# Router products moved into the scan, logits by column groups, an unsplit first gather, dummy products in waits and modulation sums on VectorE

## The chip, the cores and the metric

One core of one Trainium2 chip runs the whole kernel as one program. The metric is the device time of that core in microseconds. A run of the kernel before took 1290.3 us in the median of three (1288.49 to 1298.68). The engines are named as in the profile: PE is TensorE (PEld its weight loads), DVE is VectorE, ACT is ScalarE, POOL is GpSimd, SP is the engine that issues the DMAs.

## The reference

A trunk of two layers over one sequence of 256 tokens with 1024 channels, in float32. Each layer has a token mixer and a channel mixer, each inside a normalisation, a shift and scale that come from a condition vector, a gate and a residual.

```python
cond = silu(c)
for i in range(2):
    mod = cond @ ada_w[i] + ada_b[i]
    sh1, sc1, g1, sh2, sc2, g2 = split(mod, 6)
    h = rmsnorm(x, norm_g[i, 0]) * (1 + sc1) + sh1
    y = mla_mixer(h) if i == 0 else mamba2_mixer(h)
    x = x + g1 * y
    h = rmsnorm(x, norm_g[i, 1]) * (1 + sc2) + sh2
    y = swiglu(h) if i == 0 else moe_swiglu(h)
    x = x + g2 * y
return rmsnorm(x, final_norm)

def moe_swiglu(h):                       # 8 experts, 2 for each token
    logits = h @ w_router
    top_vals, top_idx = top_k(logits, 2)
    gates = sum(one_hot(top_idx) * softmax(top_vals))
    return sum(gates[:, e:e+1] * swiglu_e(h) for e in range(8))
```

## The kernel before

The activations stand transposed, channels on partitions: `xT` holds 8 blocks of 128 channels by 256 tokens. Weights come from HBM in pieces of 1 MB through a ring of eight buffers (`raw`, ten in the experts); every load is issued on SP's queue in the order in which a scheduler lists it, and a load waits until its buffer's last reader is done. Precise products are made of three: a weight is split by ACT and DVE (line 158) into a high and a low half, and lines 346 to 348 or 1280 multiply high by high, high by low and low by high. A float32 product is one instruction in the program and two records in the trace. The order on each engine is the scheduler's; the code's order and the releases of buffers guide it.

**The start.** The modulation of the first sub-layer is needed in units of 512 columns: units 0 and 2 are shift and scale of channel blocks 0 to 3, units 1 and 3 of blocks 4 to 7. `ada_rows` (line 246) multiplies the condition with the weights on PE, each of the eight row blocks on one of four column groups of 32, so that the result is four partial rows; DVE copies it (line 249) and `ada_columns` (line 257) turns it into columns with a column that has a one in each group (`one4`). `make_gsc` and `normmod` (lines 268, 329, 331) then give the normalised blocks `h32`, and `win_mm` (line 437) projects them: six products a block, blocks 0 to 3 first, then units 1 and 3, then blocks 4 to 7. Rows for the sine and cosine, the latents (`latent`, lines 291, 486) and attention follow. Later modulation units are summed on DVE instead (line 219), beside PE's other work.

**The scan.** Layer 1's mixer goes over four groups of heads. Two PSUM banks called `s` serve decay steps, transposes and norms, two called `in` the projections, four called `y` the output sums.

**The router.** `ssm_out` of the last group ends the mixer; its last half calls `then(m)` before each of eight blocks of output channels: `finish` adds the residual (line 364), `logits` (line 981) multiplies a block of `xT` with the router's weights, 128 tokens by 8 experts a product, `token_rows` (line 991) transposes tokens onto partitions, and ACT sums their squares (line 995). Ahead of them stand, once, the logits of the shift (line 953: the modulation as weights, 8 columns), and the gains in a layout of one column a channel (line 966), all in one `in` bank. Then come the root and reciprocal (lines 1018 to 1020), the logits with their scale (1022), the two largest and their indices (1044, 1046), the choice `sel` (1049), ranks by five thin products (1064 to 1068), positions `pos` (1070) and the selection matrix of the first expert (1084).

**The first gather.** `halves_of` scales the transposed tokens and splits them into `xt_hi` (ACT, line 1054) and `xt_lo` (DVE, line 1055); ACT copies the tokens (1103); gates and the sorting of experts by their number of tokens follow on DVE (1105 to 1146). `gather` (line 1189) multiplies high and low halves with the selection, four products of 128 columns a block; the first expert has 64 slots and takes only 64 of them, which ACT brings out with gain and shift (1197). Its weights, in float32 and without splitting, are multiplied at line 1372. Eight of its 1 MB pieces are loaded during the last scan group (`early`), two more into the ring's extra buffers behind the router; the next load waits until the first buffer has been used up. The experts follow in a fixed order of slots (64; 128 and 32; 128 and 64; 128 and 128; 32).

Of the kernel before, what the change touches and what calls it, by code (L numbers as in the profile page):

```python
# [79 lines left out]
def body(ctx: ExitStack, tc, x, c, positions, ada_w, ada_b, norm_g,  # L80
# [112 lines left out]
    few = per.tile([P, 4], F32, name="few")  # L193
    warm, halfpi, zero, one4 = (few[:, i:i + 1] for i in range(4))
# [57 lines left out]
    def ada_columns(units, rows):  # L252

        ps = pt("m")
        for i, (u, row) in enumerate(zip(units, rows)):
            for m in range(4):
                PE.matmul(ps[:, 4 * i + m:4 * i + m + 1], row[:, m * P:(m + 1) * P], one4, start=i == m == 0,
                          stop=True, skip_group_check=True)
        for i, u in enumerate(units):
            V.tensor_add(mod[:, 0, 4 * u:4 * u + 4], ps[:, 4 * i:4 * i + 4], vecT[:, 0, 4 * u:4 * u + 4])  # L260
# [116 lines left out]
    with ExitStack() as lctx:  # L377
# [13 lines left out]
        V.reduce_sum(one4, ident.rearrange("p (g q) -> p g q", g=4)[:, :, 0], axis=AX.X)  # L391
# [8 lines left out]
        win = [win_load(0, 3), win_load(3, 3)]  # L400
        aw[1] = ada_load(0, 1)
        u3 = ada_w[0, :, 1536:2048]
# [21 lines left out]
        ada_columns((0, 2), [ada_rows(aw[u]) for u in (0, 2)])  # L424
# [16 lines left out]
        ada_columns((1, 3), [ada_rows(aw[u]) for u in (1, 3)])  # L441
# [240 lines left out]
    with ExitStack() as lctx:  # L682
# [221 lines left out]

        y = st = None
        for g in range(SG):
# [32 lines left out]
            if g >= 2:  # L939
                last_gate(8 + g)  # L940
        y2 = state(SG - 1, st)
# [3 lines left out]
        make_gsc(1, 1)  # L945
        ssm_out(SG - 1, 0, *y)


        A.activation(warm, zg[:, 3, 0:1], AF.Sqrt, scale=0.0)
        V.tensor_mul(wrg, wrt, gsc[:, 1, 1, :].unsqueeze(2).to_broadcast([P, DC, NE]))  # L950
        ps_lg = pt("in")
        for k in range(DC):
            PE.matmul(ps_lg[:, 2 * NE:3 * NE], mod[:, 1, 24 + k:25 + k].to_broadcast([P, P]), wrt[:, k, :],
                      start=(k == 0), stop=(k == DC - 1), skip_group_check=True)
        V.tensor_copy(lg0, ps_lg[:, 2 * NE:3 * NE])


        scr = nrm.tile([P, 512], F32, tag="acc", name="scr")
        m24, ssq = scr[:, :24], scr[:, 32:38].rearrange("p (z j) -> p z j", z=3)
        SP.dma_start(m24, consts[:, C_EIGHTH:NCONST])  # L960
        gs8 = nrm.tile([P, 2, P], F32, tag="tt", name="gs8")
        for z, src in enumerate((gsc[:, 1, 1, :], mod[:, 1, 24:32])):
            V.tensor_tensor(gs8[:, z, :].rearrange("p (k a) -> p k a", k=DC),
                            src.unsqueeze(2).to_broadcast([P, DC, 16]),
                            m24[:, 0:16].unsqueeze(1).to_broadcast([P, DC, 16]), ALU.mult)
            PE.matmul(ps_lg[:, (3 + z) * NE:(4 + z) * NE], gs8[:, z, :], m24[:, 16:24], start=False, stop=True,
                      skip_group_check=True)
# [30 lines left out]
        def then(m):  # L998
# [4 lines left out]
            if m == 5:  # L1003
                logits(0)
            if m == 6:
                token_rows(0)
# [675 lines left out]
```

## Time and profile before

| | us |
|---|---|
| runs of the kernel, median (lowest, highest) | 1290.3 (1288.49, 1298.68) |
| profiled execution, its own time | 1296.65 |
| its span, first to last instruction | 1294.9 |
| mean granted PE clock in it | 0.967 |
| PE, DVE, ACT busy | 1220.2, 838.6, 692.0 |
| HBM read | 405.46 MB, 314 GB/s over the span |

Times in the rows below are from the start of the span. A row of a chain gives start, length and what the chain went through; a row of a timeline start, busy time, engine, line, operation, output and inputs, and in brackets the idle time before it with what ended it. A row by windows gives for each engine the busy time and, in brackets, the number of instructions, then the granted PE clock (1.00 is 2.4 GHz, 0.50 is 1.2 GHz), the share of the DMA engines and GB/s. A busy PE need not be at its peak, since products overlap.

### The profile page before, as it was taken

The numbers are of one execution on the slowest core, as the hardware profiler recorded it, in microseconds if no ns is written. First come the engines' busy times: TensorE is split into PE (matmuls) and PEld (weight loads), VectorE is DVE, ScalarE is ACT, GpSimd is POOL, SyncE is SP. The second block draws the span as 40 slices with busy tenths as digits, with TensorE's granted clock in tenths as the row PEclk, the third lists the DMA queues.
The fourth block names the chain that finished last, engine by engine and source line by source line (L and its number), as shares of the span: only waits on it lengthen the run. The fifth ranks groups of instructions, "written<-read, shape, count | busy, mean of one in ns | idle before, by whom it ended". The sixth has DMA issues, their size and how long they took to land.

```text
span 1294.9 us, 21688 instructions
## 1 busy us (share of the span) xinstructions
PE 1220.2 (94%) x8510; PEld 985.2 (76%) x8510; DVE 838.6 (65%) x1293; ACT 692.0 (53%) x1156; POOL 16.9 (1%) x16
## 2 busy tenths in 40 slices
PE   6999999999999999998999997899999999999975
PEld 4678899999989999996548884388855688888731
DVE  3377788778779788863037880288912779988412
ACT  2368554555467776634147660377703676776301
POOL 4000000000000000000000000000000000000000
PEclk8999989999989999997999998999999999999989
DMA  9786559888943356424999999999999999998895
GB/s 343 274 305 215 195 191 380 295 304 282 326 148 131 130 198 243 179 99 164 421 421 420 421 384 416 421 421 420 403 386 421 420 420 386 379 353 315 339 421 213
DMA packets 104748, 407.99 MB, mean 315 GB/s; under 512 B 10417, under 2 KB 16062, under 8 KB 70974
## 3 DMA queue, kind: packets, MB, share of 16 engines
q1 hardware_dynamic: 104638, 406.53, 81.3%
q8 instruction: 68, 1.11, 0.4%
q14 instruction: 42, 0.34, 0.1%
HBM read 405.46 MB, written 1.05 MB: 314 GB/s over the span
## 4 chain that ended last, share of the span: by engine, by line
PE 80%; DMA 11%; ACT 4%; DVE 3%; issue 1%; SPq 0%; ACTq 0%; DVEq 0%
PE a L1280 19%; PE y L1325 10%; DMA raw<-in_moe_w_down_dram 7%; PE a L1372 6%; DMA raw<-in_moe_w_up_dram 4%; PE y L346 3%; PE gu L347 3%; PE gu L346 3%; PE gu L348 3%; PE y L347 3%; PE y L348 3%; PE in L348 2%; PE in L346 2%; PE in L347 2%; PE mm L437 2%; PE mm L504 2%
## 5 line engine op out<-in xcount | busy, mean ns | idle before, releaser
L158 DVE TENSOR_TENSOR wlo<-raw,whi 128x1024 fp32r<-128x1024 f32 x395 | 466.6, 1218 | 87.9 <-ACT whi L158 86.3
L158 ACT CAST whi<-raw 128x1024 fp32r<-128x1024 f32 x395 | 404.2, 1051 | 189.7 <-PE a L1280 42.8
L1280 PE MATMUL a<-wlo,xe_hi 128*128 128x512 f32 (+1 forms) x464 | 154.3, 346 | 0.2
L1280 PE MATMUL a<-whi,xe_lo 128*128 128x512 f32 (+1 forms) x464 | 153.3, 342 | 0.0
L1280 PE MATMUL a<-whi,xe_hi 128*128 128x256 f32 (+1 forms) x464 | 111.8, 346 | 7.8 <-ACT whi L158 7.8
L219 DVE SCALAR_TENSOR_TENSOR acc<-raw,cond,acc 128x512 f32<-128x512 f32 x140 | 103.2, 748 | 3.2 <-ACT acc L217 1.5
L346 PE MATMUL gu<-hT_hi,whi 128*128 128x256 f32 x352 | 99.8, 284 | 1.2 <-ACT hT_hi L333 1.2
L1280 PEld LDWEIGHTS a<-wlo,xe_hi 128*128 128x128 f32 x464 | 87.8, 189 | 16.2 <-DVE wlo L158 3.4
L347 PE MATMUL gu<-hT_lo,whi 128*128 128x256 f32 x352 | 99.8, 284 | 0.0
L348 PE MATMUL gu<-hT_hi,wlo 128*128 128x256 f32 x352 | 99.2, 282 | 0.0
L1280 PEld LDWEIGHTS a<-whi,xe_lo 128*128 128x128 f32 x464 | 88.1, 190 | 10.0
L1280 PEld LDWEIGHTS a<-whi,xe_hi 128*128 128x128 f32 x464 | 76.4, 189 | 24.3 <-ACT whi L158 15.0
L1372 PE MATMUL a<-raw,xe 128*64 128x384 f32 (+3 forms) x640 | 81.6, 415 | 0.0
L346 PE MATMUL in<-hT_hi,whi 128*128 128x256 f32 (+1 forms) x264 | 76.0, 288 | 0.7 <-DVE r L302 0.7
L348 PE MATMUL in<-hT_hi,wlo 128*128 128x256 f32 (+1 forms) x264 | 75.5, 287 | 0.5 <-DVE wlo L158 0.5
L1293 DVE TENSOR_TENSOR sg<-sg,a 128x512 f32<-128x512 f32 (+2 forms) x30 | 18.1, 639 | 87.9 <-PE a L1372 76.0
L347 PE MATMUL in<-hT_lo,whi 128*128 128x256 f32 (+1 forms) x264 | 74.7, 283 | 0.0
L1372 PEld LDWEIGHTS a<-raw,xe 128*64 128x64 f32 x640 | 46.0, 136 | 34.6 <-issue 26.4
L1439 PE MATMUL a<-raw,xe 128*32 128x128 f32 (+1 forms) x960 | 54.6, 363 | 18.2 <-DMA raw<-in_moe_w_up_dram 18.2
L346 PEld LDWEIGHTS gu<-hT_hi,whi 128*128 128x128 f32 x352 | 67.2, 191 | 1.4 <-ACT hT_hi L333 1.4
L347 PEld LDWEIGHTS gu<-hT_lo,whi 128*128 128x128 f32 x352 | 67.3, 191 | 0.0
L348 PEld LDWEIGHTS gu<-hT_hi,wlo 128*128 128x128 f32 x352 | 67.3, 191 | 0.0
(407 smaller groups left out, 2359.6 us busy)
## 6 DMA issues: line engine op xcount, KB each, us to landing
raw<-in_moe_w_gate_dram SPq DMA_DIRECT2D x88, 1024.0 KB, 7.4
raw<-in_moe_w_up_dram SPq DMA_DIRECT2D x88, 1024.0 KB, 14.6
raw<-in_moe_w_down_dram SPq DMA_DIRECT2D x85, 1024.0 KB, 16.0
raw<-in_ada_w_dram SPq DMA_DIRECT2D x46, 1024.0 KB, 7.3
raw<-in_ssm_w_in_dram SPq DMA_DIRECT2D x20, 1024.0 KB, 5.2
raw<-in_ffn_w_down_dram SPq DMA_DIRECT2D x11, 1024.0 KB, 8.6
raw<-in_ffn_w_gate_dram SPq DMA_DIRECT2D x10, 1024.0 KB, 8.0
raw<-in_ffn_w_up_dram SPq DMA_DIRECT2D x10, 1024.0 KB, 8.8
```

The costliest lines, as they stand in the source:

```text
L158: return A.copy(hi, src), V.tensor_sub(lo, src, hi)
L219: V.scalar_tensor_tensor(acc, w[k // 4][:, k % 4, :], cond[:, k:k + 1], acc, op0=ALU.mult, op1=ALU.add)
L346: PE.matmul(ps, whi, ahi, start=(first and i == 0), stop=False, skip_group_check=skip)
L347: PE.matmul(ps, whi, alo, start=False, stop=False, skip_group_check=skip)
L348: PE.matmul(ps, wlo, ahi, start=False, stop=(last and i == n - 1), skip_group_check=skip)
L437: PE.matmul(ps, win[k // 3][:, k % 3, sl], h32[:, k, :], start=first and k == 0, stop=k == DC - 1, skip_group_check=True)
L504: PE.matmul(ps, lhs(k), rhs(k), start=(k == 0), stop=(k == n - 1))
L1280: PE.matmul(bank[:, o:o + n], a[:, j, :], w[:, m], start=f, stop=l, skip_group_check=True)
L1293: V.tensor_mul(self.sg[:, sl], self.sg[:, sl], self.acc["u", b][:, :n])
L1325: PE.matmul(self.y[b], a, w[:, b * 512:(b + 1) * 512], start=f, stop=l, skip_group_check=True)
L1372: PE.matmul(bank[64 * h:64 * (h + 1), o // 2:(o + n) // 2], self.xhi[:, j, :], w[:, h, :], start=first, stop=last, skip_group_check=True)
L1439: PE.matmul(self.acc[which, b][32 * g:32 * g + 32, o:o + m * P], self.xhi[:, j, :], w[:, first - q0::2, :, h], start=j == 0 and c % 2048 = ...
```

## The change

- The router's work that needs no token (gain times router weights, the logits of the shift, the gains in their layout) moves into the first group of the scan as `router()`, in an `s` bank. The shift's logits are summed over blocks by DVE first, so that one thin product is left of eight.
- The logits take the router's weights as the stationary side: 8 columns on one of four column groups, 256 tokens streaming, four blocks a call. The four partial sums, transposed, are copied to SBUF and folded by two thin products.
- The first gather uses the scaled tokens whole in float32 (`xt`), 64 columns, two products a block. The split into halves, the gates and their sorting go behind it.
- `keep_warm` puts products of ones with ones into waits: 34 at the start, 13 between the logits and the first gather.
- The sums of the first four modulation units go from PE to DVE, with ACT taking the first block, in two accumulators a unit; `ada_pair` (line 263) adds them in thin products. The loads are in another order: units 1 and 3 ahead of the second and third part of `w_in`.
- The PSUM banks of the experts are laid out with `y` first.

```diff
-    def ada_rows(w):
-        ps = pt("mm")
-        for k, wk in enumerate(t[:, k, :] for t in w for k in range(t.shape[1])):
-            g = k % 4 * 32
-            PE.matmul(ps[g:g + 32, :], cond[:, k:k + 1].to_broadcast([P, 32]), wk, start=k < 4, stop=k >= 4,
-                      skip_group_check=True)
-        row = nrm.tile([P, 512], F32, tag="acc", name="row")
-        V.tensor_copy(row, ps)
-        return row
+    def ada_sums(w):
+        both = hlp.tile([P, 1024], F32, tag="wlo", name="acc2")
+        acc = [both[:, z * 512:(z + 1) * 512] for z in range(2)]
         for k, wk in enumerate(t[:, k, :] for t in w for k in range(t.shape[1])):
+            a = acc[k % 2]
+            if k == 0:
+                A.activation(a, wk, AF.Copy, scale=cond[:, k:k + 1])
+            elif k == 1:
+                V.tensor_scalar(a, wk, cond[:, k:k + 1], None, op0=ALU.mult)
+            else:
+                V.scalar_tensor_tensor(a, wk, cond[:, k:k + 1], a, op0=ALU.mult, op1=ALU.add)
+        return acc
+    def ada_pair(u, sums, warm=(0, 0)):
         ps = pt("m")
+        for i, acc in enumerate(sums):
+            if warm[i]:
+                keep_warm(pt("mm"), warm[i])
+            for z in range(2):
+                for m in range(4):
+                    c = 4 * i + m
+                    PE.matmul(ps[:, c:c + 1], acc[z][:, m * P:(m + 1) * P], ones[:, 0:1],
+                              start=z == 0 and c == 0, stop=z == 1, skip_group_check=True)
...
+    def keep_warm(ps, n):
+        for _ in range(n):
+            PE.matmul(ps[:, 384:], ones, ones, start=True, stop=True, skip_group_check=True)
...
-        win = [win_load(0, 3), win_load(3, 3)]
+        win = [win_load(0, 3)]
         aw[1] = ada_load(0, 1)
-        aw[3] = [load(u3[0:512, :], 4), load(u3[512:768, :], 2), load(u3[768:1024, :], 2)]
-        win += [win_load(6, 2)]
+        aw[3] = ada_load(0, 3)
...
+        win += [win_load(3, 3), win_load(6, 2)]
...
-        ada_columns((0, 2), [ada_rows(aw[u]) for u in (0, 2)])
+        sums = ada_sums(aw[0]), ada_sums(aw[2])
+        ada_pair(0, sums, (8, 26))
...
-        ada_columns((1, 3), [ada_rows(aw[u]) for u in (1, 3)])
+        sums = ada_sums(aw[1]), ada_sums(aw[3])
+        ada_pair(1, sums)
...
+        def router():
+            make_gsc(1, 1)
+            V.tensor_mul(wrg, wrt, gsc[:, 1, 1, :].unsqueeze(2).to_broadcast([P, DC, NE]))
+            ps = pt("s")
...
+            SP.dma_start(m24, consts[:, C_EIGHTH:NCONST])
+            V.tensor_mul(by_k, wrt, mod[:, 1, 24:32].unsqueeze(2).to_broadcast([P, DC, NE]))
+            V.reduce_sum(sums, by_k.rearrange("p k n -> p n k"), axis=AX.X)
+            PE.matmul(ps[:, 0:NE], ones, sums, start=True, stop=True)
...
+            V.tensor_copy(lg0, ps[:, 0:NE])
+            V.tensor_copy(gain8, ps[:, NE:3 * NE].rearrange("p (z e) -> p z e", z=2))
...
         def logits(k0):
-            for k in (k0, k0 + 1):
-                for j in range(2):
-                    PE.matmul(ps_lg[:, j * NE:(j + 1) * NE], xT[:, k, j * P:(j + 1) * P], wrg[:, k, :],
-                              start=False, stop=(k == DC - 1), skip_group_check=True)
+            for i in range(4):
+                PE.matmul(ps_lg[32 * i:32 * i + NE, 0:S], wrg[:, k0 + i, :], xT[:, k0 + i, :], start=k0 == 0,
+                          stop=k0 > 0, skip_group_check=True)
...
+        token_rows(6)
         logits(4)
-        token_rows(6)
-        logits(6)
+        lgT = nrm.tile([P, S], F32, tag="tt", name="lgT")
+        V.tensor_copy(lgT, ps_lg[:, 0:S])
         V.tensor_add(ssq[:, 0, :], ssq[:, 0, :], ssq[:, 1, :])
+        dim = pt("y")
+        keep_warm(dim, 2)
+        for j in range(2):
+            PE.matmul(ps_lg[:, S + j * NE:S + (j + 1) * NE], lgT[:, j * P:(j + 1) * P], fold, start=True, stop=True,
+                      skip_group_check=True)
+        keep_warm(dim, 8)
...
+    for (q, j), ps in pst.items():
+        A.activation(xt[:, j, :, q * 64:(q + 1) * 64], ps.rearrange("t (p c) -> t c p", c=DC), AF.Copy,
+                     scale=rtok[:, j:j + 1])
...
+    keep_warm(dim, 3)
...
-    for cc in range(DC):
-        gather(xs, psel, cc, True)()
+    for c0 in (0, 4):
+        ps = pt("a").rearrange("p (c t) -> p c t", c=4)
+        for cc in range(c0, c0 + 4):
+            for j in range(2):
+                PE.matmul(ps[:, cc - c0, 0:n0], xt[:, j, cc, :], sel0[:, j, :], start=j == 0, stop=j == 1,
+                          skip_group_check=True)
+        for cc in range(c0, c0 + 4):
+            A.activation(xs[0][0][:, cc, :], ps[:, cc - c0, 0:n0], AF.Identity, bias=gain8[:, 1, cc:cc + 1],
+                         scale=gain8[:, 0, cc:cc + 1])
```

On DVE at the start, before, where `row` is the copied modulation row and `tt` a normalised block ahead of its shift:

```order
L709 CAST ej<-cst 128x128 x2
L415 RECIPROCAL r<-r 128x2
L210 COPY vecT<-n 128x128
L249 COPY row<-mm 128x512 x2
L260 TENSOR_TENSOR mod<-m,vecT 128x4 x2
L268 SCALAR_TENSOR_TENSOR gsc<-mod,vecT 128x4
L329 SCALAR_TENSOR_TENSOR tt<-xT,gsc,n 128x256 x2
```

On DVE at the same place now, where `acc_182` and `acc_191` are the accumulators of units 0 and 2, `acc_294` and `acc_303` of units 1 and 3:

```order
L720 CAST ej<-cst 128x128 x2
L249 TENSOR_SCALAR acc_182<-raw,cond 128x512
L424 RECIPROCAL r<-r 128x2
L251 SCALAR_TENSOR_TENSOR acc_182<-raw,cond,acc_182 128x512
L210 COPY vecT<-n 128x128
L251 SCALAR_TENSOR_TENSOR acc_182<-raw,cond,acc_182 128x512 x5
L249 TENSOR_SCALAR acc_191<-raw,cond 128x512
L251 SCALAR_TENSOR_TENSOR acc_191<-raw,cond,acc_191 128x512 x6
L266 TENSOR_TENSOR mod<-m,vecT 128x2x4
L210 COPY vecT<-n 128x21
L279 SCALAR_TENSOR_TENSOR gsc<-mod,vecT 128x4
L340 SCALAR_TENSOR_TENSOR tt<-xT,gsc,n 128x256 x4
```

Two copies have become fourteen passes over 512 columns ahead of the first `mod`.

On PE behind the last output products of the scan, before (`in` is the bank of the logits, `sel` the choice):

```order
L981 MATMUL in<-wrg,xT 128x8 x6
L991 MATMUL in<-cst,xT 128x128
L991 MATMUL y<-cst,xT 128x128
L991 MATMUL in<-cst,xT 128x128
L991 MATMUL y<-cst,xT 128x128
L981 MATMUL in<-wrg,xT 128x8 x2
L1064 MATMUL y<-sel,uones 128x8
L1065 MATMUL y<-sel,uones 128x8
L1066 MATMUL y<-sel,uones 128x8
L1067 MATMUL y<-sel,uones 128x8
L1068 MATMUL y<-sel,uones 128x8
L1189 MATMUL a<-psel,xt_hi 128x128
```

On PE at the same place now (`lgT` is the copied transposed logits, `scr` holds the fold matrix, `ones` rows are the dummies):

```order
L999 MATMUL in<-xT,wrg 8x256 x3
L271 MATMUL y<-ones 128x128 x3
L1039 MATMUL in<-scr,lgT 128x8 x2
L271 MATMUL y<-ones 128x128 x7
L1086 MATMUL y<-sel,uones 128x8
L1087 MATMUL y<-sel,uones 128x8
L1088 MATMUL y<-sel,uones 128x8
L1089 MATMUL y<-sel,uones 128x8
L1090 MATMUL y<-sel,uones 128x8
L271 MATMUL y<-ones 128x128 x3
L1503 MATMUL a<-psel,xt 128x64 x16
```

The last group of logits is four products (three stand in its row here, one ahead of the transposes) instead of eight, ten dummies and the fold stand in front of the choice's products and three behind them, and the gather is sixteen products of 64 columns instead of 32 of 128.

## Rows read from the trace of the kernel before

**Rows 1.** The page's chain of waits, shares of the span by engine

```profile
PE 80%; DMA 11%; ACT 4%; DVE 3%; issue 1%; SPq 0%; ACTq 0%; DVEq 0%
```

**Rows 2.** By windows, around the router and in the first expert

```profile
577.00:582.20 5.20, 5.20 (x33) 5.19 (x32) 1.79 (x5) 0.00 (x0) 0.00 (x0) 0.68 0.02 3
...
592.50:602.70 10.20, 8.72 (x37) 8.19 (x37) 8.52 (x40) 7.53 (x17) 0.00 (x0) 0.50 0.68 256
602.70:606.20 3.50, 3.50 (x11) 1.01 (x12) 0.00 (x0) 1.69 (x2) 0.00 (x0) 0.50 0.00 0
...
625.00:650.00 25.00, 25.00 (x193) 14.99 (x191) 3.09 (x9) 3.61 (x11) 0.00 (x0) 1.00 1.01 420
```

**Rows 3.** The chain of waits through the router and the first expert

```profile
575.73 1.68 PE in L953 x16
...
583.11 0.79 PE in L981 x8
...
590.29 0.57 ACT junk L995 x3
...
591.67 0.36 DVE lg L1022 x2
...
592.78 0.18 DVE sel L1049
...
594.27 0.18 DVE pos L1070
...
594.68 0.28 DVE psel L1084
...
595.68 7.11 PE a L1189 x31
602.79 41.52 PE a L1372 x317
...
648.76 19.83 DMA raw<-in_moe_w_down_dram
```

**Rows 4.** Timeline of SP: the first load that needs a used buffer

```profile
606.39 0.33 SPq L132 DMA_DIRECT2D raw<-in_moe_w_gate_dram  x1
```

**Rows 5.** The chain of waits at the start

```profile
23.12 14.84 PE mm L437 x48
37.96 2.71 PE mm L246 x24
...
43.51 1.07 PE m L257 x8
...
46.21 9.84 PE mm L437 x36
```

**Rows 6.** By windows, at the start

```profile
8.00:22.00 14.00, 12.11 (x70) 6.82 (x69) 2.45 (x9) 5.38 (x10) 5.57 (x7) 1.00 1.05 391
...
24.00:29.00 5.00, 5.00 (x12) 2.92 (x12) 0.00 (x0) 0.52 (x2) 0.00 (x0) 0.50 1.05 384
...
46.00:50.00 4.00, 3.79 (x10) 3.06 (x11) 3.79 (x13) 1.46 (x4) 0.00 (x0) 0.57 1.05 392
```

**Rows 7.** Groups by line: the logits (count, busy us, mean ns, idle)

```profile
L981 PE MATMUL in<-wrg,xT 128*128 128x8 f32 x32 | 3.8, 245 | 0.0
```

**Rows 8.** Timeline of ACT behind the reciprocal

```profile
591.60 1.26 ACT L1054 ACTIVATE xt_hi<-s,rtok 128x512 fp32r<-128x512 f32 x2 [0.23 <-DVE rtok L1020]
...
593.89 1.09 ACT L1103 COPY x_tok<-s 128x512 f32<-128x512 f32 x2
...
596.92 1.28 ACT L1106 ACT_TABLE_LOAD   x1
```

**Rows 9.** One line's instructions: DVE's step of a modulation sum (ns least, median, most)

```profile
L219 DVE SCALAR_TENSOR_TENSOR acc<-raw,cond,acc x140: 732/748/803, 67.3 to 514.1; 128x512 f32<-128x512 f32 x140
```

**Rows 10.** Timeline at the start: ACT's copies, PE's wait for unit 2

```profile
11.87 1.54 ACT L421 COPY xT<-mm 128x512 f32<-128x512 f32 x3
...
18.64 0.14 PEld L246 LDWEIGHTS mm<-raw,cond 128*32 128x32 f32 x4 [0.42 <-DMA raw<-in_ada_w_dram]
```

More of the change, by code (lines that the diff above doesn't have):

```diff
@@ L192, in body @@
     V.memset(eps_t, EPS)
-    few = per.tile([P, 4], F32, name="few")
-    warm, halfpi, zero, one4 = (few[:, i:i + 1] for i in range(4))
+    few = per.tile([P, 3], F32, name="few")
+    warm, halfpi, zero = few[:, 0:1], few[:, 1:2], few[:, 2:3]
     V.memset(zero, 0.0)
@@ L940, in body @@
                 last_gate(8 + g)
+            if g == 0:
+                router()
         y2 = state(SG - 1, st)
@@ L944, in body @@
         y = y2
-        make_gsc(1, 1)
         ssm_out(SG - 1, 0, *y)
         A.activation(warm, zg[:, 3, 0:1], AF.Sqrt, scale=0.0)
[L950 to L955, printed above, removed]
-        scr = nrm.tile([P, 512], F32, tag="acc", name="scr")
[L959 to L967, printed above, removed]
-        V.tensor_copy(gain8, ps_lg[:, 3 * NE:5 * NE].rearrange("p (z e) -> p z e", z=2))
+        scr = nrm.tile([P, 512], F32, tag="acc", name="scr")
+        ssq, fold = scr[:, :6].rearrange("p (z j) -> p z j", z=3), scr[:, 8:8 + NE]
+        V.reduce_sum(fold, ident.rearrange("p (g q) -> p q g", g=4)[:, 0:NE, :], axis=AX.X)
         pst = {}
@@ L1135, in body @@
     by_rank(pos_s, pos)
-    by_rank(gates_s, gates)
-    split(ej[:, :, S:S + NE], ej[:, :, S + NE:S + 2 * NE], gates_s)
     cmx = ep.tile([P, 1], F32, name="cmx")
@@ L1180, in gathered, with gather @@
                 ew.tile([P, DC, P], F32R, tag="xe_lo", name="xe_lo"))
-    def gather(xs, sel2, cc, first=False):
+    def gather(xs, sel2, cc):
         m = len(xs) * P
@@ L1499, in body @@
     xs = [gathered(0)]
-    for cc in range(DC):
-        gather(xs, psel, cc, True)()
+    n0 = SLOTS[ORDER[0][0]]
+    sel0 = psel.bitcast(F32)[:, :, 0, 0:n0]
+    for c0 in (0, 4):
[3 more added lines that the diff above has]
+                PE.matmul(ps[:, cc - c0, 0:n0], xt[:, j, cc, :], sel0[:, j, :], start=j == 0, stop=j == 1,
+                          skip_group_check=True)
+        for cc in range(c0, c0 + 4):
+            A.activation(xs[0][0][:, cc, :], ps[:, cc - c0, 0:n0], AF.Identity, bias=gain8[:, 1, cc:cc + 1],
+                         scale=gain8[:, 0, cc:cc + 1])
+    V.tensor_sub(wts[:, :, 0:1], top[:, :, 1:2], top[:, :, 0:1])
+    A.activation(wts[:, :, 1:2], wts[:, :, 0:1], AF.Exp)
+    V.tensor_scalar(wts[:, :, 0:1], wts[:, :, 1:2], 1.0, None, op0=ALU.add)
+    V.reciprocal(wts[:, :, 2:3], wts[:, :, 0:1])
+    V.tensor_mul(wts[:, :, 3:4], wts[:, :, 1:2], wts[:, :, 2:3])
+    for j in range(2):
+        V.tensor_scalar(gates[:, j, :], m12[:, j, 0, :], wts[:, j, 2:3], None, op0=ALU.mult)
+        V.scalar_tensor_tensor(gates[:, j, :], m12[:, j, 1, :], wts[:, j, 3:4], gates[:, j, :],
+                               op0=ALU.mult, op1=ALU.add)
+    by_rank(gates_s, gates)
+    split(ej[:, :, S:S + NE], ej[:, :, S + NE:S + 2 * NE], gates_s)
+    for j in range(2):
+        A.copy(xt_hi[:, j, :, :], xt[:, j, :, :])
+        V.tensor_sub(xt_lo[:, j, :, :], xt[:, j, :, :], xt_hi[:, j, :, :])
     SP.dma_start(fn_row, bcast(final_norm, D))
```

72 lines of the change are left out of this document (23 added, 49 removed).

## The prediction

> **What bounds the kernel now.** I read the chain of waits first: PE holds 80% of it, DMA 11% [rows 1]. Both come to the same statement about time: nearly everything before the experts is PE in sequence, and behind the router the weight stream and PE go on together. So a stretch counts only if PE or the stream stands still in it, or PE runs slowly. A table by windows, read second, finds three such stretches around the router: PE's clock has a mean of 0.68 from 577.0 to 582.2, is 0.50 (the lower of its two levels, 1.2 GHz) from 592.5 to 602.7, and is 0.50 still to 606.2, while the DMA engines rest completely in that last window [rows 2]. Later the stream runs at 420 GB/s [rows 2], and the first expert ends in a 19.8 us wait for weights [rows 3]. That is why the router is worth its whole length: all buffers are full, the next weight load is issued at 606.39, when the first buffer has been used up [rows 4], and whatever moves that issue moves the stream and all that hangs on it.
>
> The fourth place is the start. There PE carries the chain from 23.12 on, but 8.3 us of it (37.96 to 46.21) are modulation rows, their column products and the way back to the next normalised block [rows 5], and two stretches have a mean clock of 0.50 and 0.57 [rows 6].
>
> **Frame.** The profiled execution took 1296.65 us, 1294.9 of them span. The sum below is of differences inside it. The median of the runs shown is 1290.3, 6.35 lower; I carry the differences over to that median unchanged.
>
> **The router, up to the choice of experts.** Sixteen thin records of the shift logits leave PE's path: 1.68 us [rows 3]. Four more (the gains) at the same 0.105 each leave: 0.4. They go into the scan (below). Behind them the clock falls: 5.2 us at a mean of 0.68 are 1.66 us lost [rows 2]. With dense products in their place I let that go: 1.6. The logits were 32 thin records [rows 7] at 0.79 us for eight [rows 3], 3.2 in all. They become eight products of 256 columns, two groups of four, each on a column group of its own. The modulation rows before are of that form, 24 records of 512 columns in 2.71 us [rows 5], so 0.9 for a group of four products (eight records) and 0.45 for one half as wide. The second group is broken by transposes and by the last residual; I charge 1.4 together, which saves 1.8. Serial they would be 3.6 (a product of 256 columns has two records of about 0.22: 36 in 9.84 us [rows 5], 3.6 us of them at half clock), a loss of 0.4. The fold is new: copy of the transposed logits (0.4), dummies, two thin products (0.4), handovers (0.3). It stands beside the last squares, the root and the reciprocal, which take from 590.29 to 591.67 [rows 3]; the two paths end within 0.2 us of each other, and I charge 0.2 (0 to 1). Together 2.1 + 1.6 + 1.8 - 0.2 = 5.3 us until the choice is made.
>
> The Trainium skill, "TensorEngine Tiling (Array Packing)", section Key Properties, says that a change of tiling mode drains TensorE, which speaks against logits in column groups between full-width products. The rows show no gap at such a change: the 32-column rows start in the chain at 37.96, exactly where the full-width products end (23.12 + 14.84) [rows 5]. If each of some five changes cost 0.2 us, what DVE stands between two of its steps at 594.45 [rows 3], the forecast below would be 1.0 us later; by the rows it stays.
>
> **From the choice to the first gather.** Before, the choice ends at 592.96 and the gather's unbroken run begins at 595.68: 2.7 us. DVE's own steps in it, positions and selection, are 0.18 and 0.28 [rows 3]; the rest is five thin products at half clock and the low halves of the gathered rows, which DVE takes in between. The low halves go. What stays is the thin products at full clock (0.5), handovers (0.3), positions 0.2, one small copy 0.1, the selection 0.4: 1.5. Gain 1.2.
>
> **The gather.** 32 products of 128 columns at half clock were 7.1 us [rows 3]. Now 16 float32 products of 64 columns, 32 records, at the 0.1 us of a thin record at full clock [rows 3]: 3.4 to 3.5. No row shows this form; at half clock it would be 6.8. ACT is a second limit: four scalings of 0.63, four copies of 0.55, a table load of 1.28 and an exponential stand before its first evacuation [rows 8], 6.6 us from the reciprocal. That ends 0.2 behind PE's way, so I credit 3.4.
>
> **The first buffer.** From 602.79 [rows 3] to the next issue at 606.39 [rows 4] are 3.6 us at half clock, so 1.8 at full: gain 1.8. The sum of the router is 5.3 + 1.2 + 3.4 + 1.8 = 11.7 us; the issue that stands at 606.39 would come near 594.7. Gates, the split of the gathered rows and the final part of the sorting move behind the gather; the first expert keeps PE 41 us before it needs them, so that cover is ample, and if it were gone their DVE and ACT work would cost about 5 us.
>
> **In the scan.** Six thin records (0.65 us) go onto PE, which is the bound there. The four small DVE products, one reduction and two copies stand between weight splits that wait for ACT or PE, and I count them as hidden; without that cover they are 1.7 us. The load of the 24 constants moves forward in SP's queue, in front of weight loads that wait for buffers in any case. Charge 0.7 (0.4 to 2.5).
>
> **The start.** The sums now run on DVE: seven steps a unit, 748 ns each as the same step elsewhere [rows 9], and ACT's step in front. ACT is free at 13.41 [rows 10]; plus about 0.6 for its step, 14.0. Then 0.3 + 6 x 0.75 for unit 0 and 7 x 0.75 for unit 2: 24.05. The last of these weights lands at 18.64 [rows 10], so DVE sets it, not the transfer. A last thin group 1.07 [rows 5], then the way from there to PE (44.58 to 46.21, 1.63 [rows 5]) and a small copy: first product at 26.9, where it was 23.12. That is a loss of 3.8. DVE starts the second pair at about 28.9 and ends it at 38.65. PE has three chunks before that, 36 records, not 48: 7.7 us at full clock, 11.1 at the mean of 14.84 for 48 [rows 5], so it is done at 34.6 to 38.0. Then come 32 thin records, the last eight behind DVE. PE is free for the fourth chunk at 40.0 to 42.2, I take 41.0, and done with it at 43.8. The old kernel is at the same point at 46.21. Gain 2.4: a later first half repaid by work that stands beside PE instead of on it. The second and third part of the projection's weights now stand behind all modulation weights; at 384 GB/s [rows 6] some 11.5 MB behind the input land near 38, 3 us before they are needed. Late next is ACT: PE comes to the first sum of squares near 49, and ACT, with a table load of 1.28 [rows 8] and sine and cosine in front, has the squares near 50; for that I credit no more than 2.4. Bounds: with no fall of the clock at either place of rows 6, +5.3; with the lower level throughout, a loss of 18 (third rival). The 18 dummies start at 13.5 and end by 17.5 at full clock, ahead of the sum they wait with, so they cost nothing; at half clock they end at 21 and do.
>
> **Sum.** 11.7 + 2.4 - 0.7 = 13.4; 1290.3 - 13.4 = **1276.9 us**. All behind the first expert is shifted as a whole, since the stream, its buffers and PE start it in the state they had before.
>
> **Rivals.** (1) The clock falls in the wait for the choice all the same. For it: it fell there before; against it: 13 dummies now stand in those gaps. Then the ten dummies in front of the choice take 4.3 us instead of 2.1 in waits of 3.0 (1.3 late), the last three and the thin products 0.9 more, the gather loses 3.4 and the first buffer 1.8: 7.4, so 1284.3. (2) The start does not repay: DVE's sums at 0.8 and the lower level through all three chunks before the second pair make 3 us of loss out of 2.4 of gain: 1282.3. (3) Slower: the dummies do not hold the clock at the start, but cost PE twice as much. Decided at 13.5 us: if the lower level is granted then, 18 dummies end at 21.2, the first product comes at 31.6, 36 records take 15.4, the fourth chunk ends at 56 instead of 46, and the remaining 48 records take 8 more: 18 lost, and with the tail of rival 1: 1290.3 + 18 + 0.7 - 4.3 = 1304.7. Against it: the clock holds through the transposes and rows at that place before, to 22 us the mean is 1.00 [rows 6]. (4) Better: both falls at the start are spared and the scan hides its part: 1277 less 3.6, 1273.
>
> **How the numbers follow.** Forecast 0.50 (its own range 1272 to 1281, 0.62 of it below 1277.4), better 0.17, rival 1 0.18, rival 2 0.10, rival 3 0.05. About 1% (1277.4 and 1303.2) is what a measurement of this kernel can tell from no change. Faster by more: 0.31 + 0.17 = 0.48; within: 0.19 + 0.18 + 0.10 = 0.47; slower: 0.05. The range 1269 to 1288 takes in the better case and rivals 1 and 2 with their spread and leaves out under 2 in 10.
>
> **What would show it.** The first expert's first product about 10 us earlier relative to the last scan product; clock 1.00 between the choice and there; no window without DMA traffic behind it; two clusters of four 32-row logit products at 0.5 us; first product of the input projection near 27 us, its fourth chunk done near 44. Wrong if the first gather takes near 7 us, if the dummies show up in the chain of waits, if the stretch from the first expert on is longer than before by more than 2 us, or if PE waits in the scan for the router's bank.

## The result, and the profile after

| | before | changed kernel |
|---|---|---|
| median of the runs (lowest, highest), us | 1291.37 (1288.49, 1298.68) | 1278.04 (1275.74, 1281.92) |
| profiled execution, its span, us | 1296.65, 1294.9 | 1275.74, 1274.0 |
| mean granted PE clock in it | 0.967 | 0.980 |

The ratio is 0.9889 with a 95% interval of 0.9853 to 0.9924: 14.3 us less, 9.8 to 19.0. The medians lie 13.3 apart, and 13.4 was forecast. A second series gave 1278.98 against 1292.81, ratio 0.9898 (0.9863 to 0.9934).

The two profiled executions lie 20.9 us apart, more than the medians, so their spans alone cannot be compared. They are cut into stages at instructions that both have, and a second trace of the changed kernel stands beside them ("again"). Where a row names an instruction, the number is its start; all others are lengths. The end of attention is the start of the last high-by-high product of its output, the choice the start of `sel`. All in us.

| stage | before | changed | again | difference (mean) | forecast |
|---|---|---|---|---|---|
| first product of the input projection | 23.12 | 25.81 | 26.26 | +2.9 | +3.8 |
| first product of its fifth chunk | 46.21 | 44.34 | 44.74 | -1.7 | -2.4 |
| last product of the projection | 60.54 | 56.98 | 57.38 | -3.4 | -2.4 |
| from there to the end of attention | 100.0 | 97.7 | 98.5 | -1.9 | 0 |
| from there to the scan | 208.7 | 205.5 | 207.3 | -2.3 | 0 |
| the scan's projections, first to last | 181.7 | 184.2 | 181.9 | +1.4 | +0.7 |
| from there to the choice | 41.8 | 36.7 | 36.7 | -5.1 | -5.3 |
| choice to the gather's unbroken run | 2.9 | 2.4 | 2.4 | -0.5 | -1.2 |
| the gather | 7.0 | 3.7 | 3.7 | -3.4 | -3.4 |
| first expert's start to the next load's issue | 3.7 | 2.1 | 2.1 | -1.6 | -1.8 |
| from there to the second expert | 65.8 | 65.3 | 65.8 | -0.3 | 0 |
| from there to the end | 622.7 | 619.3 | 619.3 | -3.3 | 0 |

The router's four rows give -10.6 where 11.7 was forecast, and every one has the forecast's sign. Nearly 8 us stand in stages for which nothing was forecast (-1.9, -2.3, -0.3 and -3.3); the part on the start says what the first of them is, the last section what is known of the others.

The page's chain of waits of the changed kernel, shares of the span by engine, answers to [rows 1]:

```profile
PE 80%; DMA 10%; ACT 4%; DVE 4%; issue 2%; SPq 0%; DVEq 0%; ACTq 0%
```

By windows, the changed kernel from the last logits to the first expert; columns as in [rows 2]:

```profile
577.40:581.20 3.80, 3.80 (x32) 2.78 (x31) 1.94 (x15) 2.42 (x8) 0.00 (x0) 1.00 0.19 41
581.20:583.60 2.40, 1.72 (x17) 1.56 (x15) 0.79 (x6) 2.40 (x5) 0.00 (x0) 1.00 1.02 258
583.60:587.30 3.70, 3.70 (x34) 3.63 (x34) 3.46 (x25) 3.36 (x8) 0.00 (x0) 1.00 1.01 416
587.30:589.70 2.40, 2.40 (x13) 0.91 (x14) 0.85 (x5) 2.32 (x7) 0.00 (x0) 1.00 0.33 140
```

The clock is 1.00 in all four, where it was 0.50 from the choice to the first used buffer, and the DMA engines no longer rest fully: the last window is 2.4 us long with a share of 0.33, against 3.5 us with none [rows 2].

The chain of waits of the changed kernel through the router, as in [rows 3], and the timeline of SP at the load that needs a used buffer, as in [rows 4]:

```profile
577.37 0.53 PE in L999 x2
...
578.26 0.54 PE in L999 x6
578.80 0.86 PE y L271 x6
579.67 0.35 PE in L1039 x4
580.01 1.66 PE y L271 x14
...
582.02 0.11 PE y L1090
582.13 0.79 PE y L271 x6
582.92 0.02 issue
582.94 0.17 DVE pos L1093
...
583.59 3.75 PE a L1503 x32
```

```profile
589.33 0.33 SPq L132 DMA_DIRECT2D raw<-in_moe_w_gate_dram  x1
```

Line 999 is the logits, 271 the dummies, 1039 the fold, 1090 the last thin product of the choice, 1503 the gather. One row shows a flaw of the change: three dummies (six records, 0.79 us) stand between the last thin product and `pos`. `pos` reads the bank that they write, so it waits for them.

The chain at the start of the changed kernel, as in [rows 5]:

```profile
22.30 1.96 PE m L263 x16
...
25.81 10.57 PE mm L447 x36
36.38 3.46 PE m L263 x32
39.85 9.40 PE mm L447 x34
```

Three chunks run, then the column products of the second pair, then the fourth chunk.

### The profile page after: what moved, and what is told of

The parts are those of the page before. It is cut to its first block, busy times and chain, and to the rows that moved or that the text cites. A ratio compares the mean times of both kernels' runs of the same rounds, so it can differ in the third digit from the quotient of the medians.

```text
span 1274.0 us, 21781 instructions
## 1 busy us (share of the span) xinstructions
PE 1202.9 (94%) x8546; PEld 980.2 (77%) x8546; DVE 856.3 (67%) x1317; ACT 698.0 (55%) x1162; POOL 18.3 (1%) x16
## 4 chain that ended last, share of the span: by engine, by line
PE 80%; DMA 10%; ACT 4%; DVE 4%; issue 2%; SPq 0%; DVEq 0%; ACTq 0%
PE a L1277 18%; PE y L1322 10%; PE a L1369 6%; DMA raw<-in_moe_w_down_dram 5%; DMA raw<-in_moe_w_up_dram 4%; PE y L357 3%; PE gu L357 3%; PE gu L358 3%; PE gu L359 3%; PE y L358 3%; PE y L359 3%; PE y L1388 3%; PE in L359 2%; PE in L357 2%; PE in L358 2%; PE mm L447 2%
## 5 line engine op out<-in xcount | busy, mean ns | idle before, releaser
L158 ACT CAST whi<-raw 128x1024 fp32r<-128x1024 f32 x395 | 404.5, 1053 | 182.2 <-PE a L1277 39.6
L1290 DVE TENSOR_TENSOR sg<-sg,a 128x512 f32<-128x512 f32 (+2 forms) x30 | 18.2, 642 | 80.2 <-PE a L1369 68.4
```

Of the source, the lines that this page charges most:

```text
L158: return A.copy(hi, src), V.tensor_sub(lo, src, hi)
L1290: V.tensor_mul(self.sg[:, sl], self.sg[:, sl], self.acc["u", b][:, :n])
```

## Experiments

A difference "by the ratio" is (ratio - 1) times the median of before in the same series, with the ends of its interval.

**The start alone.** The kernel before with `ada_sums`, `ada_pair`, the 34 dummies and the new order of loads; the router as before.

```diff
-        ada_columns((0, 2), [ada_rows(aw[u]) for u in (0, 2)])
+        sums = ada_sums(aw[0]), ada_sums(aw[2])
+        ada_pair(0, sums, (8, 26))
```

> The kernel before with the change's start alone (sums on VectorE and ACT, pairs, 34 dummies, order of loads); the router stays as before. Theory A (the start repays by its own work): by the prediction 2.4 us less than before, by the changed kernel's trace 4.2 less at the end of the projections, so 1287 to 1289 against 1291.4. Rival B (what the trace shows at the start is only where the clock fell in that execution): within 1 us of before, and the fourth chunk of the projection not earlier than 46 us when the clock falls in it.

1288.85 against 1291.52, ratio 0.9983 (0.9965 to 1.0001): -2.2 us, -4.5 to +0.1. The trace repeats the changed kernel's: last projection product at 57.07, end of attention at 155.95. The trace bears out theory A: the clock fell at 40.4 us, in the fourth chunk, and that chunk was done at 44.4, ahead of the 46 that rival B allows. The time alone does not tell the start's effect from none.

**The router alone.** The changed kernel with the old start (`ada_rows`, `ada_columns`, loads as before).

> The changed kernel with the old start. Theory A (the router's terms, 11.7 less 0.7 in the scan): 11 us less than before, 1280.4. Rival B (the router gives about 8 and the start more than forecast): 1283. In its trace the first weight load that needs a used buffer should be issued about 11 us earlier behind the last output product of the scan than the 18.4 of before.

1282.68 against 1291.52, ratio 0.9932 (0.9907 to 0.9957): -8.8 us, -12.0 to -5.5. Both theories lie in the interval. By its trace the issue of that load comes 12.7 us behind the last output product of the scan instead of 18.4. That is 5.7 earlier, not 11: I had put the mark at the wrong place, since the rest of the gain lies ahead of it, where the stretch from the last projection is 32.2 instead of 37.0. The two are 10.5 together, nearer to A. Both parts together are 11.0 by the ratios, so the two halves of the change add up about to the whole.

**Dummies alone, in the kernel before.** Ten behind the last logits, three behind the choice's thin products.

```diff
         logits(6)
+        dim = pt("y")
+        keep_warm(dim, 10)
...
+    keep_warm(dim, 3)
     V.tensor_mul(pos, ps[:, :2 * NE].rearrange("p (j n) -> p j n", j=2), sel)
```

> The kernel before with 10 dummy products behind the last logits and 3 behind the five thin products of the choice, nothing else. Theory A (at least half of the router's gain is the clock that these waits let fall): the gather's run 3.5 us instead of 7.1, the first buffer used up in 1.8 instead of 3.6, the thin products 0.6 less, the positions 0.3 late: 5.5 us less than before, 1286. Rival B (the removed work carries the gain, dummies only keep a number up): within 1 us of before, the gather still near 7.

1291.62 against 1291.52, ratio 1.0007 (0.9987 to 1.0028). Rival B by the time, but not by its reason: by windows, the clock fell all the same.

```profile
589.00:591.50 2.50, 1.49 (x11) 1.30 (x11) 2.17 (x7) 2.37 (x5) 0.00 (x0) 1.00 1.01 254
591.50:599.30 7.80, 7.43 (x32) 7.05 (x32) 6.30 (x33) 5.05 (x12) 0.00 (x0) 0.50 0.62 252
```

The gather runs in the second window, at 0.50. Dummies alone buy nothing here. The fall of the kernel before ahead of its last output product (the window with a mean of 0.68 in [rows 2]) did not come in this trace, though the 16 thin records of the shift stand in it and every dummy stands behind them.

**The changed kernel without these dummies.** `keep_warm(dim, 2)`, `(dim, 8)` and `(dim, 3)` are taken out.

> The changed kernel without its 13 dummies behind the logits. Theory A (they hold the clock): the granted clock falls to 0.50 between the choice and the first expert, the gather takes 6.8 to 7.5 instead of 3.75 and the first buffer 1.5 to 1.8 more, the positions come 0.8 earlier: 4 to 5 us more than the changed kernel, 1282.5. Rival B (with the shorter waits the clock holds without them): 0.8 less than the changed kernel, 1277.2, since the positions no longer wait for the last three.

1283.64 against 1291.52, ratio 0.9939 (0.9920 to 0.9959): -7.9 us, 5.3 to 6.4 us less gain than the changed kernel's two series. By windows, gather and first buffer:

```profile
581.50:588.10 6.60, 6.60 (x32) 6.50 (x32) 5.16 (x27) 5.01 (x10) 0.00 (x0) 0.53 0.77 313
588.10:592.20 4.10, 4.10 (x11) 1.22 (x12) 1.40 (x2) 2.63 (x7) 0.00 (x0) 0.50 0.00 0
```

Theory A: 32 records in 6.6 us instead of 3.7. From the last output product to the second expert it takes 82.3 us instead of 77.9 (78.5 in the second trace). So the same 13 products are worth 4.4 us in the changed kernel and nothing in the old one. What differs?

**The changed kernel with thin logits.** Tokens as the stationary side again, 32 records of 8 columns, no fold.

```diff
-                PE.matmul(ps_lg[32 * i:32 * i + NE, 0:S], wrg[:, k0 + i, :], xT[:, k0 + i, :], start=k0 == 0,
-                          stop=k0 > 0, skip_group_check=True)
+                for j in range(2):
+                    PE.matmul(ps_lg[:, S + j * NE:S + (j + 1) * NE], xT[:, k0 + i, j * P:(j + 1) * P],
+                              wrg[:, k0 + i, :], start=k0 + i + j == 0, stop=k0 + i == DC - 1, skip_group_check=True)
```

> The changed kernel with the logits as 32 thin records again (tokens stationary, 8 columns), without the fold, dummies and all else as changed. Theory A (dummies held the clock here, and not in the kernel before with the same dummies, because the logits are 256 columns wide): the clock falls to 0.50 before the gather, the gather takes about 7, the first product of the second expert stands 4 us later behind the last output product, and the logits themselves cost 1.8 more. Rival B (the difference was the wait for the halves in the old gather): the clock holds, the gather takes 3.7, only the logits' 1 to 2 us are lost, less 0.5 for the fold.

1285.78 against 1291.51, ratio 0.9961 (0.9941 to 0.9981). By windows:

```profile
587.50:589.90 2.40, 1.49 (x11) 1.33 (x12) 0.81 (x6) 2.40 (x6) 0.00 (x0) 1.00 0.91 265
589.90:596.80 6.90, 6.90 (x32) 6.79 (x32) 4.15 (x28) 3.56 (x8) 0.00 (x0) 0.51 0.67 280
```

Rival B is out: no halves stand in front of this gather, and it takes 6.9 us at 0.51. From the last output product to the second expert it takes 84.5 us instead of 77.9 (84.2 in the kernel before), and the choice stands 38.7 us behind the last projection of the scan instead of 36.7: the thin form itself costs 2.0.

The fall is as theory A has it, but not its reason alone, since the edit changes a second thing. Without the fold the ten dummies run out before the choice is made. Timelines of the first product behind the choice: this run, dummies alone, changed kernel:

```profile
587.73 0.27 PE L1082 MATMUL y<-sel,uones 128*128 128x8 f32 x1 [0.75 <-DVE sel L1069]
```

```profile
589.38 0.27 PE L1071 MATMUL y<-sel,uones 128*128 128x8 f32 x1 [0.64 <-DVE sel L1056]
```

```profile
581.43 0.25 PE L1086 MATMUL y<-sel,uones 128*128 128x8 f32 x1
```

Both runs whose clock fell have a wait of 0.64 to 0.75 us there beside the wait for the selection (0.68 us in all three). In the changed kernel the fold holds the dummies back, and they fill the time up to the choice. Whether the 256 columns or the closed wait held the clock is not shown; no run with these dummies has one without the other.

With 256-column logits in front, the clock held in all but one of the eight traces that leave the router as changed, or change in it only the bank of the last dummies or the column groups of the logits. In the one (the run without dummies at the start) it fell 2.7 us into the gather, so this router does not hold it every time.

**Logits on one column group.** `ps_lg[0:NE, 0:S]` takes all eight blocks, one behind the other.

> The changed kernel with its logits on one column group, the eight blocks summed one behind the other. Theory A (four column groups overlap, as the prediction charged 1.4 us for all against 3.6 in sequence at half clock): the two clusters of eight records take 1.8 us together instead of 1.1, about 0.7 more to the choice at full clock. Rival B (a change of the tiling drains TensorE at each of some five places): the same or up to 0.3 less.

A single run, 1283.14 against 1292.81. The chain of waits at the last six records and the first dummies:

```profile
582.57 1.39 PE in L999 x6
583.96 0.87 PE y L271 x6
```

1.39 us against 0.54 on four groups, and the choice comes 0.86 later behind the last output product. The first eight records stand ahead of that mark. Timelines of both ends of that cluster, changed kernel and this run:

```profile
572.42 0.28 PE L358 MATMUL y<-ylo,whi 128*128 128x256 f32 x1
572.54 0.28 PE L359 MATMUL y<-yhi,wlo 128*128 128x256 f32 x1
572.75 0.62 PE L999 MATMUL in<-xT,wrg 128*8 128x256 f32 x8
```

```profile
575.78 1.89 PE L999 MATMUL in<-xT,wrg 128*8 128x256 f32 x8
577.61 0.66 PE L1009 MATMUL s<-cst,xT 128*128 128x128 f32 x4
```

They take 1.89 us instead of 0.62. From the last projection to the choice it is 38.8 us instead of 36.7: 2.1 lost, theory A with three times its 0.7, and as much as with thin logits (38.7). So the time saved by the logits is that of the four column groups; 256 columns on one group save none. The clock held here all the same.

The rows also price a change between full-width and grouped products, by starts. Full-width products of 256 columns begin 0.12 us apart, the first grouped one 0.21 behind the last of them; grouped records on one column group begin 0.22 apart, the first full-width one 0.31 behind the last of them. That is 0.09 us a change, and for the six changes around the three groups of logits an estimate of 0.5 us. The Trainium skill's rule that a change of tiling mode drains TensorE ("TensorEngine Tiling (Array Packing)", Key Properties) agrees with these 0.09 us. The chain shows no gap there because a product's start lies ahead of the end of the one before it (572.75 against 572.82).

**The first gather split again.** High and low halves by copy and subtraction from `xt`, 32 products of 128 columns.

```diff
+    for j in range(2):
+        A.copy(xt_hi[:, j, :, :], xt[:, j, :, :])
+        V.tensor_sub(xt_lo[:, j, :, :], xt[:, j, :, :], xt_hi[:, j, :, :])
+    for cc in range(DC):
+        gather(xs, psel, cc)()
```

> The changed kernel with the first gather in high and low halves again (32 products of 128 columns; the halves are made by copy and subtraction from the scaled tokens), everything else as changed. Theory A (the gather got shorter by the clock, not by the form, since both forms are 32 thin records; what the unsplit form saves is the halves on ACT and VectorE in front): the gather's run at full clock about 3.5 to 4 once it runs, but begun 3 to 4 us later, behind copy and subtraction, and the wait may let the clock fall (then 7): 3 to 8 us more than the changed kernel. Rival B (the form itself halves the time): 7 us at a granted clock of 1.00.

1286.33 against 1291.51, ratio 0.9965 (0.9948 to 0.9983): about 9 us less gain than the changed kernel, where 3 to 8 were expected. Chain of waits:

```profile
588.15 1.14 DVE xt_lo L1499
589.33 6.09 PE a L1189 x27
```

The first product stands 8.6 us behind the last output product instead of 6.9, the last low half holds PE to 589.33, and the clock falls at 589.0. Timeline of PE at the start of the gather:

```profile
587.00 0.77 PE L1189 MATMUL a<-psel,xt_hi 128*128 128x128 f32 x5 [2.36 <-ACT xt_hi L1498]
589.33 0.48 PE L1189 MATMUL a<-psel,xt_lo 128*128 128x128 f32 x1 [1.56 <-DVE xt_lo L1499]
```

The five records at full clock begin 0.11 us apart (0.16 the first), those behind the fall 0.21. So 32 of the split form would be about 3.6 us at full clock (an estimate from these steps), where the unsplit ones take 3.7: the form is no shorter, and what it saves is the wait in front. Theory A.

**No dummies at the start.** `ada_pair(0, sums)`.

> The changed kernel without the 34 dummies at the start. Theory A (they hold the clock through the wait for VectorE's sums): the clock falls before 24 us already and the three chunks take 2 to 4 us more, so the projection ends 2 to 4 us later than 57.0 to 57.4. Rival B (the clock falls behind the first pair with and without them, as it did at 24 to 27 us in every trace of the new start): no difference at the end of the projection, within 0.7 us.

1282.19 against 1291.51, ratio 0.9924 (0.9893 to 0.9956): 3.4 to 4.5 us less gain than the changed kernel, with intervals that overlap. By windows, this run:

```profile
14.00:18.00 4.00, 1.26 (x6) 1.26 (x7) 3.93 (x7) 0.72 (x1) 0.00 (x0) 0.64 1.06 388
18.00:22.00 4.00, 2.41 (x12) 2.33 (x12) 3.84 (x6) 0.00 (x0) 0.00 (x0) 0.50 1.03 386
22.00:25.00 3.00, 3.00 (x15) 3.00 (x15) 0.00 (x0) 0.00 (x0) 0.00 (x0) 0.50 1.05 386
```

The changed kernel has 1.00 in the same three windows. The 16 thin records of unit 2 take 3.57 us at half clock instead of 1.96, the first projection product stands at 27.09 and the last at 59.02 instead of 56.98 and 57.38, 1.6 to 2.0 later: theory A at its lower end. In this trace the clock also falls into the gather, and from the last output product to the second expert it takes 81.2 us instead of 77.9 and 78.5, so not all of the lost time is the start's.

**The last three dummies in a bank of their own.** So that they keep their place, the choice is their stationary side.

```diff
-    keep_warm(dim, 3)
+    held = sel.bitcast(F32).rearrange("p j n -> p (j n)")
+    dim = pt("y")
+    for _ in range(3):
+        PE.matmul(dim[0:2 * NE, 384:], held, ones, start=True, stop=True, skip_group_check=True)
```

> The changed kernel with the last three dummies in a bank of their own, the choice as their stationary side so that they stand where they stood. Theory A (the positions wait for these three, since they share a bank): the positions come 0.75 us earlier behind the choice (1.0 instead of 1.78), the gather begins 0.7 earlier, the clock holds, 0.7 us less than the changed kernel. Rival B (with the dummies beside them the positions are early, but 16 columns as stationary side don't hold the clock): the gather near 7 us, 3 to 4 more than the changed kernel.

1278.86 against 1292.81, ratio 0.9889 (0.9860 to 0.9917), beside 0.9898 in the same series. The time cannot tell 0.7 us apart, but the trace can. Chain of waits:

```profile
580.22 0.11 PE y L1090
580.33 0.76 PE y L1095 x6
581.09 3.76 PE a L1506 x32
```

The dummies (line 1095) still lead to the gather in the chain, but positions and selection now run beside them: `pos` stands 1.01 us behind the choice, not 1.78, the gather 6.16 behind the last output product, not 6.89, the clock holds: theory A.

**Additions for the second pair, dummies at the first gain.** The accumulators of units 1 and 3 are added on DVE ahead of the column products; four products with `gsc` as stationary side follow the gain.

```diff
+        if one:
+            V.tensor_add(acc[0], acc[0], acc[1])
+            return acc[:1]
...
+            PE.matmul(keep[0:4, 384:], gsc[:, 0, 0, 0:4], ones, start=True, stop=True, skip_group_check=True)
```

> The changed kernel with the two accumulators of units 1 and 3 added on VectorE ahead of the column products (16 thin records fewer on TensorE, two additions of about 0.5 us more on VectorE), and four dummies behind the first gain. Theory A (thin products and waits in which the clock falls are what is left at the start): the second pair's column products end 1.2 to 1.6 us earlier, the falls at 26 and 40 us go (1.7 each): 2 to 4 us less than the changed kernel at the end of the projection. Rival B (VectorE is late with the second pair, and its additions lengthen the wait): 0.5 us less to 1 more.

1277.44 against 1292.81, ratio 0.9866 (0.9831 to 0.9902). The clock fell at 24.2, ahead of the four dummies, which then took 1.86 us and held the first projection product to 26.29, though its block was ready near 25.4. The second pair's products end at 38.63 instead of 39.85 and 40.30, but a fall of 6.8 us stands at 37.8, and the last projection product at 57.06 is no earlier. The end of attention at 153.49 is 1.2 and 2.3 us earlier. A mixed answer: the column products are shorter by the additions, and these dummies cost. The end of attention is earlier without an earlier end of the projection; how much of that is the additions' is not shown.

**The two that helped.** Dummies in their own bank, additions for the second pair.

> The changed kernel with two edits that the runs point to: the last three dummies in a bank of their own, as in the run on them, and the accumulators of units 1 and 3 added on VectorE, without the four dummies at the first gain. Theory A: first product of the projection at 25.4 to 26.3 as in the changed kernel, the second pair's column products ended 1.2 earlier and about 2 us less up to the end of attention, positions 1.0 behind the choice, 10.5 - 0.7 = 9.9 us from the last output product to the first expert; 2 to 3 us less than the changed kernel, 1275 to 1276.5. Rival B (what stands earlier at the start waits again for VectorE or ACT before attention): 0.7 less, 1278.

1274.50 against 1292.10, ratio 0.9859 (0.9841 to 0.9876): -18.2 us, -20.5 to -16.0, and the shortest median of all runs, 3.9 to 5.0 us below the changed kernel's two series where 2 to 3 were expected. Its interval overlaps that of the changed kernel (-19.0 to -9.8). Chain of waits at the start:

```profile
25.14 11.86 PE mm L450 x36
37.00 1.68 PE m L266 x16
38.68 7.76 PE mm L450 x34
```

Sixteen thin records instead of 32, the last projection product at 54.17, the end of attention at 152.59, `pos` 1.01 behind the choice: theory A.

## Why the prediction was right

**The total.** 13.4 us forecast, 13.3 between the medians. It is the sum of a router term a little too large, a start term too small and a scan term a little too small, so part of the agreement is luck: the terms as found (10.6 + 3.4 - 1.1) make 12.9, and the interval of the measured gain is 9 us wide.

**Router up to the choice: 5.3 forecast, 5.1 found.** Three traces split it, by the way from the last projection to the choice: 41.8 us before, 40.7 with dummies alone (no fall of the clock, worth 1.5, of which 0.4 are given back behind the last output product), 38.7 with thin logits (the shift's thin records gone too), 36.7 as changed. That is 1.1 for the fall, 2.0 for the thin products and 2.0 for the logits, where 1.6, 2.1 and 1.8 less 0.2 for the fold were charged. That the thin records make the clock fall, as the term supposes, is shown in part only: two of the three traces with them have the fall, none of the eleven without. That a change to column groups leaves no gap is a misreading of rows 5, whose pieces follow without one because products overlap: there too the first grouped product begins 0.31 us behind the last full-width one, where those begin 0.22 apart. At 0.09 us a change this is half of the 1.0 us that the text allowed.

**Choice to gather: 1.2 forecast, 0.5 found.** This step failed. "What stays is the thin products at full clock (0.5), handovers (0.3) ... the selection 0.4: 1.5" left out the last three dummies, which I had put "in those gaps". They stand in the way of `pos`, as the chain shows with 0.79 us; in a bank of their own the positions came 0.77 earlier behind the choice, the missing gain. The text's own sign for "wrong", dummies in the chain of waits, did come.

**Gather 3.4 and first buffer 1.8: 3.4 and 1.6 found.** They are the clock's gain, and the run without dummies gives both back (6.6 us, and 3.7 from the first expert's start to the next load's issue). What I had not seen is what the dummies need. I argued "13 dummies now stand in those gaps" and gave rival 1 a chance of 0.18. The dummies alone did not hold the clock, nor did they with thin logits: there they left a gap of 0.64 to 0.75 us ahead of the choice. So the logits with their fold are worth more than their own 2.0 us: with them the dummies held the clock in seven of eight traces. Which part of that form does it, the columns or the dummies' later place, stays open.

**Start: 2.4 forecast, 3.4 found at the end of the projection.** The term was mis-sized in its last step. First product and fourth chunk came 2.9 late and 1.7 early (forecast 3.8 and 2.4), but "for that I credit no more than 2.4" was wrong: chunks five to eight take 12.6 us instead of 14.3, because the fall behind the old wait for the next block [rows 6] now lies in the fourth chunk. That fall of 3.4 us at half clock is worth 1.7, the whole difference. All three traces of the old start have a fall in these chunks, and the eleven of the new start lose at most 0.25 us to one there. So half of the 3.4 is shorter work and half is where the clock falls. ACT, which the text feared, is no limit: its sine and cosine are done at 45.9, where they stood at 54.5 to 55.3. The 1.9 us of the next stage come of falls too: the trace before has two of 3.4 us in it (at 63 and 142), the changed kernel's none and one. Rivals 2 and 3 fell: the 24 steps of the sums took 0.73 to 0.75 us, not 0.8, and the clock was 1.00 from 10 to 25 us.

**Scan: 0.7 charged.** The one trace with the old scan and no fall behind its first 6 us (dummies alone) has 181.2 us; the eight with the router's products and no such fall have 181.5 to 182.2, a mean of 181.9. That is 0.7, but from one trace. Every trace also enters the scan in a fall, of different length. With half of the low-clock time taken off, the three old scans have 177.6 to 178.3 us and the eleven new ones 178.0 to 179.3: 1.1 between the means. In three of the eleven the clock falls for 6.8 us at 442 to 447 and the scan takes 184.2 to 185.8; in the three without these products it does not fall there, though in two of them it falls for 3.4 us at 419 to 425. Whether the moved products have a part in it stays open.

## What to carry to other kernels

A dummy product is worth what it keeps at full clock, and only with the work around it: price it by the stretch behind it, and test it alone and without it. It must not write a bank that the next step reads, since that step then waits for it. Look for the gap that the dummies leave: here 0.64 to 0.75 us ahead of the choice went with a fall of the clock in both runs that had them. Thin products on four column groups in a form with many columns saved 2.0 us; the same form on one group saved nothing.

## What the runs showed of the hardware that was not expected

TensorE has two paces at a granted clock of 1.00. By windows, the same stage of the channel mixer, before, changed kernel and again (the first bracket of a row is the number of products):

```profile
240.00:300.00 60.00, 59.86 (x519) 59.46 (x518) 45.98 (x58) 31.22 (x59) 0.00 (x0) 1.00 0.87 324
```

```profile
240.00:300.00 60.00, 59.91 (x527) 59.50 (x526) 46.95 (x59) 31.71 (x64) 0.00 (x0) 1.00 0.83 306
```

```profile
240.00:300.00 60.00, 59.87 (x509) 59.47 (x508) 44.82 (x57) 31.09 (x63) 0.00 (x0) 1.00 0.80 292
```

PE is busy throughout and the clock is 1.00 in all three, yet 527 products go through in one execution and 509 in another. In the timelines the products of 256 columns follow each other every 118 ns, and in some stretches every 113; where these stretches lie differs between executions of one kernel. The mixer's gate and up products, first to last, take 173.8 us in the first trace of the changed kernel and 176.6 in the second, with a fall of 6.8 us at the start of each. The pace and the falls of the clock, which come at other places in each execution, account for the stage from attention to the scan. From the second expert to the end the fourteen traces have 618.6 to 622.7 us, with the three of the old router at 619.7, 621.8 and 622.7: the 3.3 us of the table lie within that spread, and no cause is shown for them. A few us between two traces are no finding; stages cut at common instructions and seen in several traces are.
